# Layer norms whose mean and 1/deviation stay in PSUM, with the whole norm on VectorE and the rotary embedding of the folded halves behind it

## The chip, the cores and the metric

The kernel runs on one core of a Trainium2 chip. The metric is device time in microseconds (us), from the start of the kernel to its end. Five engines work side by side, each through its own queue in order: TensorE (PE; its weight loads are listed as PEld), VectorE (DVE), ScalarE (ACT), GpSimd (POOL) and SyncE (SP), which here only issues loads. An engine waits where its next instruction needs something that another has not finished. [...]

## The reference: one inference step of a two-layer decoder

288 tokens (256 of a prompt, 8 sequences of 4 new tokens) go through two layers of width 1024 in float32. Each layer is

```
proj = x @ w_in                        # 768 q, 768 k, 768 v, 2 x 256 of the gate
q, k = rope(q), rope(k)                # rotary embedding of 16 of 64 dimensions
mix  = [dilated window attention (3 groups of 4 heads, with caches), spatial gate]
x = layer_norm(alpha * x + mix @ w_mix_out)
x = layer_norm(alpha * x + cross_attention(x @ w_xq, memory) @ w_xo)
x = layer_norm(alpha * x + square(relu(x @ w_up)) @ w_down)

def layer_norm(x, g, b):               # over the 1024 features of a token
    mu, var = mean(x), mean((x - mu) ** 2)
    return (x - mu) / sqrt(var + 1e-5) * g + b
```

## The kernel before

Activations lie transposed: 8 tiles of 128 features by 288 tokens. `linear` walks over tiles of 256 columns of a weight matrix, two halves of 128 columns each. Weights and inputs are split into a high part (rounded to the fast matmul format) and the rest, and a half-tile is 24 matmuls into one PSUM bank `acc`: high by high, low by high and high by low, for each of 8 feature tiles (L336 to L338). `acc` has three banks, used in turn, so half-tile n waits until the evacuation of half n-3 has read its bank. ScalarE makes the high part `wh` of the weights (L318), VectorE the low part `wl` (L319); three buffers of each, so they run two halves ahead.

A layer norm needs all 1024 features before its first output. So the linear behind it starts with **folded** halves, which run on (z - c) * g, not normalised yet (`fH`, `fL`), with c a first estimate of the mean; two more columns give the terms in g and b, hence 290 columns. `LN.stats` multiplies the sums with a matrix of ones (L562, L563), so that every partition has mean and mean square; ScalarE copies the mean to SBUF (`s`, L565) and makes 1/deviation (`q`, L569, L570). `LN.fold` then evacuates a folded half: `fw` is copied out of the bank (L501), `fy` = s * fw + acc on VectorE (L502, the last to read the bank), and `fy` *= q (L505), on GpSimd for the first four of a norm and on VectorE later. `LN.apply` makes the normalised x itself: subtract the mean (L577, tiles in turn on VectorE and GpSimd), scale by g and 1/deviation (L581, VectorE), high part `xH` and the shift by b on ScalarE (L584, L586), low part `xL` on VectorE (L591).

There are five such norms: ahead of `w_xq` in both layers (xq norm: all eight halves folded, and no `xH` or `xL` made), ahead of `w_up` in both (up norm: three tiles, six halves folded) and ahead of `w_in` of the second layer (w_in norm: two tiles, four halves folded; these are queries). In `w_in` the evacuation of q and k halves ends with the rotary embedding: shuffle and product on VectorE (L671, L672), product and sum on GpSimd (L673, L674). From the rotated queries of a group ScalarE makes `zq`, `zn`, and a `query` goes by memory (`qd`, `qb`) onto the partitions of the cached keys, where VectorE and GpSimd multiply them (L1009, L1007).

The order on each engine comes from a scheduler that interleaves such tasks by priorities and modelled latencies; `behind` holds an instruction back until an urgent one has been queued (`gates`).

## Time and profile before

| | us |
|---|---|
| median of 3 runs | 1097.1 (1093.85 to 1100.27) |
| span of the profiled execution | 1090.5, 6.6 below the median of the runs |
| PE busy | 1045.1 (96%) |
| DVE busy | 767.2 (70%) |
| ACT busy | 534.1 (49%) |
| POOL busy | 191.2 (18%) |
| means issued (L562) | 170.71, 329.61, 538.71, 709.82, 868.50 |

The profile shows one execution. The span runs from the first to the last instruction; no other time of that execution is given. The five times in the last row are where the norms stand: xq, up, w_in, xq, up.

### The profile page before, as it was taken

What the parts mean: (1) busy time and instruction counts of PE and PEld (TensorE: products, weight loads), DVE (VectorE), ACT (ScalarE), POOL (GpSimd) and SP (SyncE); (2) the same over time, 40 slices, a digit from 0 to 9 for tenths busy, and PEclk for the clock granted to TensorE, in tenths of its full rate; (3) what the DMA queues carried; (4) which work ended last, traced back from release to release, by engine and by line L of the source; (5) the groups of instructions that cost most, each with busy time, mean ns of one, the idle gap of its engine ahead of it and who ended that gap; (6) DMA issues with size and microseconds to landing.
All of it is one profiled execution on the core that took longest, in us unless ns stands there. A gap on an engine that the chain in (4) does not pass through costs nothing. (4 is left out here: it accounts for less than half of the span.)

```text
span 1090.5 us, 20141 instructions
## 1 busy us (share of the span) xinstructions
PE 1045.1 (96%) x8038; PEld 957.0 (88%) x8038; DVE 767.2 (70%) x1406; ACT 534.1 (49%) x1000; POOL 191.2 (18%) x151
## 2 busy tenths in 40 slices
PE   8989999999999999999978998999999999999995
PEld 7979599878898999999968885997788999999995
DVE  6688689755479756565998876895554997565656
ACT  4437456544457535353553373674343585354432
POOL 5592022000023000000469300220000320000000
PEclk9999999999999999999989999999999999999998
DMA  9988955687854655545446869456865555555531
GB/s 291 303 249 280 244 185 189 205 256 236 299 160 136 194 161 186 156 157 172 136 128 214 250 209 265 155 192 201 276 209 206 155 146 184 160 171 183 182 117 43
DMA packets 185533, 213.68 MB, mean 196 GB/s; under 512 B 5760, under 2 KB 175136, under 8 KB 185440
## 3 DMA queue, kind: packets, MB, share of 16 engines
q1 hardware_dynamic: 177216, 205.00, 59.9%
q10 hardware_dynamic: 8224, 7.41, 2.1%
q8 instruction: 63, 1.03, 0.4%
q14 instruction: 30, 0.25, 0.1%
HBM read 203.80 MB, written 8.59 MB: 195 GB/s over the span
## 5 line engine op out<-in xcount | busy, mean ns | idle before, releaser
L318 ACT ACTIVATE wh<-wraw 128x1024 fp32r<-128x1024 f32 (+1 forms) x237 | 249.4, 1054 | 294.9 <-PE acc L337 218.8
L319 DVE TENSOR_TENSOR wl<-wraw,wh 128x1024 fp32r<-128x1024 f32 (+1 forms) x237 | 309.1, 1306 | 113.2 <-ACT wh L318 112.1
L336 PE MATMUL acc<-xH,wh 128*128 128x288 f32 x728 | 218.5, 301 | 6.8 <-DVE fy L502 6.8
L338 PE MATMUL acc<-xH,wl 128*128 128x288 f32 x728 | 217.5, 299 | 3.3 <-DVE wl L319 3.3
L337 PE MATMUL acc<-xL,wh 128*128 128x288 f32 x728 | 217.5, 299 | 0.0
L336 PE MATMUL acc<-hH,wh 128*128 128x288 f32 x512 | 151.3, 296 | 0.0
L337 PE MATMUL acc<-hL,wh 128*128 128x288 f32 x512 | 151.2, 295 | 0.0
L338 PE MATMUL acc<-hH,wl 128*128 128x288 f32 x512 | 150.9, 295 | 0.0
L336 PEld LDWEIGHTS acc<-xH,wh 128*128 128x128 f32 x728 | 138.6, 191 | 8.2 <-issue 5.2
L338 PEld LDWEIGHTS acc<-xH,wl 128*128 128x128 f32 x728 | 138.5, 191 | 4.8 <-DVE wl L319 4.2
L337 PEld LDWEIGHTS acc<-xL,wh 128*128 128x128 f32 x728 | 138.6, 190 | 1.0 <-DVE fy L726 0.4
L520 POOL TENSOR_TENSOR s<-s,xres 128x288 f32<-128x288 f32 x15 | 20.3, 1353 | 464.4 <-DVE s L516 463.9
L336 PEld LDWEIGHTS acc<-hH,wh 128*128 128x128 f32 x512 | 96.3, 188 | 0.0
L337 PEld LDWEIGHTS acc<-hL,wh 128*128 128x128 f32 x512 | 96.3, 188 | 0.0
L338 PEld LDWEIGHTS acc<-hH,wl 128*128 128x128 f32 x512 | 96.2, 188 | 0.0
L336 PE MATMUL acc<-fH,wh 128*128 128x290 f32 x256 | 78.1, 305 | 1.8 <-DVE fy L502 1.8
L337 PE MATMUL acc<-fL,wh 128*128 128x290 f32 x256 | 77.0, 301 | 0.0
L338 PE MATMUL acc<-fH,wl 128*128 128x290 f32 x256 | 75.7, 299 | 0.5 <-DVE wl L319 0.5
L336 PEld LDWEIGHTS acc<-fH,wh 128*128 128x128 f32 x256 | 48.3, 189 | 2.6 <-PE acc L338 2.2
L337 PEld LDWEIGHTS acc<-fL,wh 128*128 128x128 f32 x256 | 48.5, 190 | 0.9 <-DVE fL L494 0.2
L338 PEld LDWEIGHTS acc<-fH,wl 128*128 128x128 f32 x256 | 48.1, 189 | 1.2 <-DVE wl L319 1.0
L1007 POOL TENSOR_TENSOR cu<-cu,qb 128x1024 f32<-128x1024 f32 x15 | 44.1, 2956 | 11.1 <-DMA qb<-qd 10.7
(318 smaller groups left out, 2199.4 us busy)
## 6 DMA issues: line engine op xcount, KB each, us to landing
cu<-cache_mem_kv SPq DMA_DIRECT2D x64, 512.0 KB, 6.2
wraw<-w_up SPq DMA_DIRECT2D x32, 1024.0 KB, 5.5
wraw<-w_down SPq DMA_DIRECT2D x32, 1024.0 KB, 4.9
cu<-cache_kv_w SPq DMA_DIRECT2D x48, 512.0 KB, 6.4
wraw<-w_in SPq DMA_DIRECT2D x21, 1024.0 KB, 6.7
wraw<-w_xkv SPq DMA_DIRECT2D x16, 1024.0 KB, 5.6
wraw<-w_mix_out SPq DMA_DIRECT2D x8, 1024.0 KB, 6.0
wraw<-w_xq SPq DMA_DIRECT2D x8, 1024.0 KB, 5.0
```

The costliest lines, as they stand in the source:

```text
L318: S.activation(h[:, r], raw[:, r], AF.Copy)
L319: gates[f"split{k}"] = behind(V.tensor_sub(lo[:, r], raw[:, r], h[:, r].bitcast(F32)), "dve")
L336: m = T.matmul(ps, wh[:, k], H[:, k], start=first, stop=False)
L337: T.matmul(ps, wh[:, k], L[:, k], start=False, stop=False)
L338: T.matmul(ps, wl[:, k], H[:, k], start=False, stop=last)
L520: eng.tensor_add(self.s, self.s, xres[:, n])
L1007: G.tensor_mul(cu, cu, qb[g])
```

## The change

Mean and 1/deviation stay in the PSUM tiles that the statistics make (`pd`, `pq`, now of the pool `dec`, which has two banks, and no longer of `tr`), and 1/deviation is written there by ScalarE. GpSimd no longer takes part: all eight subtractions and every fold's multiplication are VectorE's. `apply` is no longer a generator that hands on tile by tile: it issues all subtractions, all scalings with `xH`, then all `xL`, which now come straight from x + b - xH. The shift of x by b comes two tiles later (`shift_back`). In `w_in` the evacuations' second part (bias and rotary embedding) of the folded halves is held until all of `apply` is issued. The first half on `xH` takes its matmuls in another order, low part of x last. The scores of the decode attention wait for `apply`, since they use the other `dec` bank.

```diff
     def linear(name, l, k0, tiles, H, L, N, evac, norm=None, folded=0, apply_at=1, ks=range(KT)):
+        held = []
         for i, c in enumerate(tiles):
             if i == apply_at and folded:
-                for _ in norm.todo:
-                    pass
+                norm.apply(H, L)
+            if i == folded:
+                for args in held:
+                    evac(*args)
+            if i == apply_at + 2 and folded:
+                norm.shift_back()
...
+                elif i == folded and not a and folded:
+                    for j, (u, v) in enumerate(((wt[0], h), (wt[1], h), (wt[0], lo))):
+                        for k in range(KT):
+                            T.matmul(p[:, :cols], u[:, k], v[:, k], start=(j + k == 0), stop=(j + k == KT + 1))
...
-                    evac(2 * c + a, *norm.fold(p))
+                    args = (2 * c + a, *norm.fold(p))
+                    if name == "w_in":
+                        held.append(args)
+                    else:
+                        evac(*args)
...
         def fold(self, ps):
...
-            self.folds += 1
-            (G if self.folds <= FOLD_POOL else V).tensor_mul(e, e, self.q)
+            V.tensor_mul(e, e, self.rstd)
...
         def stats(self):
-            pd, pq = tr(), tr()
-            T.matmul(pd[:, :TOK], ones, self.s, start=True, stop=True)
-            gates["pe"] = T.matmul(pq[:, :TOK], ones, self.q, start=True, stop=True)
-            m2, rstd = self.c, self.q
-            S.activation(self.s, pd[:, :TOK], AF.Copy)
-            S.activation(m2, pd[:, :TOK], AF.Square)
-            gates["dve"] = V.scalar_tensor_tensor(out=m2, in0=pq[:, :TOK], scalar=EPS, in1=m2,
+            pd, pq = dec("pd"), dec("pq")
+            self.mean, self.rstd = pd[:, :TOK], pq[:, :TOK]
+            T.matmul(self.mean, ones, self.s, start=True, stop=True)
+            gates["pe"] = T.matmul(self.rstd, ones, self.q, start=True, stop=True)
+            m2 = self.c
+            S.activation(m2, self.mean, AF.Square)
+            gates["dve"] = V.scalar_tensor_tensor(out=m2, in0=self.rstd, scalar=EPS, in1=m2,
                                                   op0=ALU.add, op1=ALU.subtract)
+            S.activation(self.s, self.mean, AF.Copy)
             S.activation(m2, m2, AF.Ln)
-            gates["act"] = S.activation(rstd, m2, AF.Exp, scale=-0.5)
+            S.activation(self.rstd, m2, AF.Exp, scale=-0.5)

         def apply(self, H, L=None):
...
-            for i in range(KT + 2):
-                if i < KT:
-                    (V if i in SUB_V else G).tensor_sub(xres[:, i], xres[:, i], self.s)
-                n = i - 1
-                if 0 <= n < KT:
...
+            for n in range(KT):
+                if n in SUB_V:
+                    behind(V.tensor_sub(xres[:, n], xres[:, n], self.mean), "dve")
...
+            for n in range(KT):
+                x, b = xres[:, n], lncol(j, 1, l, n)
+                V.scalar_tensor_tensor(out=x, in0=x, scalar=lncol(j, 0, l, n), in1=self.rstd,
+                                       op0=ALU.mult, op1=ALU.mult)
+                if H is not None:
+                    S.activation(H[:, n], x, AF.Identity, bias=b)
+            if L is not None:
+                for n in range(KT):
+                    V.scalar_tensor_tensor(out=L[:, n], in0=xres[:, n], scalar=lncol(j, 1, l, n),
+                                           in1=H[:, n].bitcast(F32), op0=ALU.add, op1=ALU.subtract)
+            tasks.flag("applied", 0)
+
+        def shift_back(self):
+            for n in range(KT):
+                S.activation(xres[:, n], xres[:, n], AF.Identity, bias=lncol(self.j, 1, self.l, n))
...
         def decode_scores():
-            sc = dec("sc")
...
+            yield "applied"
+            sc = dec("sc")
```

How this moves instructions shows in the order of the queues. Line numbers differ between the two kernels (L502 is L512 in the changed one, L319 L317, L581 L593, L577 L588, L591 L599).

The first place is VectorE's queue in the up norm of the first layer. Before, the evacuations of the folded halves two to four (of `acc_3903`, `acc_3984`, `acc_4023`) stand right behind the scalings and ahead of every low part `xL`:

```order
L581 SCALAR_TENSOR_TENSOR xres_103<-xres_103,lnp_155,q_3506 128x288 x8
L501 COPY fw_3928<-acc_3903 128x2
L319 TENSOR_TENSOR wl_3981<-wraw_3746,wh_3980 128x1024
L1383 TENSOR_TENSOR r_3870<-r_3870 128x288
L501 COPY fw_4009<-acc_3984 128x2
L502 SCALAR_TENSOR_TENSOR fy_3929<-s_3505,fw_3928,acc_3903 128x288
L319 TENSOR_TENSOR wl_4020<-wraw_3746,wh_4019 128x1024
L1384 TENSOR_TENSOR hL_3833<-r_3870,hH_3832 128x288
L501 COPY fw_4048<-acc_4023 128x2
L502 SCALAR_TENSOR_TENSOR fy_4010<-s_3505,fw_4009,acc_3984 128x288
L502 SCALAR_TENSOR_TENSOR fy_4049<-s_3505,fw_4048,acc_4023 128x288
```

In the changed kernel the queue, from the low parts on, reads so up to the evacuation of the fourth folded half, now `acc_4015`:

```order
L512 SCALAR_TENSOR_TENSOR fy_4002<-s_3505,fw_4001,acc_3976 128x288
L317 TENSOR_TENSOR wl_4053<-wraw_3834,wh_4052 128x1024
L599 SCALAR_TENSOR_TENSOR xL_3831<-xres_103,lnp_155,xH_3830 128x288
L1397 TENSOR_TENSOR r_3933<-r_3933 128x288
L599 SCALAR_TENSOR_TENSOR xL_3831<-xres_103,lnp_155,xH_3830 128x288 x3
L511 COPY fw_4081<-acc_4056 128x2
L599 SCALAR_TENSOR_TENSOR xL_3831<-xres_103,lnp_155,xH_3830 128x288
L514 TENSOR_TENSOR fy_4002<-fy_4002,pq_3822 128x288
L317 TENSOR_TENSOR wl_4092<-wraw_3834,wh_4091 128x1024
L599 SCALAR_TENSOR_TENSOR xL_3831<-xres_103,lnp_155,xH_3830 128x288 x3
L1398 TENSOR_TENSOR hL_3833<-r_3933,hH_3832 128x288
L511 COPY fw_4120<-acc_4095 128x2
```

The row behind these twelve is `fy_4041`, which reads `acc_4015` (and the rows ahead of them are the scalings, eight in a row). The fourth evacuation has moved from ahead of the low parts to behind all eight of them and two more `wl`; its bank is the one that the seventh half, the first on `xH`, takes.

The second place is VectorE's queue in the w_in norm. Before, each rotary embedding (`ro`) stands between the evacuations, and the fourth (`fy_6331`) behind three of them and four low parts:

```order
L671 STREAM_SHUFFLE ro_6213<-fy_6207 128x288
L672 TENSOR_TENSOR ro_6212<-fy_6207,const_63 128x288
L502 SCALAR_TENSOR_TENSOR fy_6290<-s_5550,fw_6289,acc_6264 128x288
L591 TENSOR_TENSOR xL_6124<-xres_103,xH_6123 128x288 x3
L726 TENSOR_SCALAR fy_6290<-fy_6290,fw_6289 128x288
L591 TENSOR_TENSOR xL_6124<-xres_103,xH_6123 128x288
L671 STREAM_SHUFFLE ro_6296<-fy_6290 128x288
L672 TENSOR_TENSOR ro_6295<-fy_6290,const_63 128x288
L502 SCALAR_TENSOR_TENSOR fy_6331<-s_5550,fw_6330,acc_6305 128x288
```

In the changed kernel the evacuations two to four (`fy_6199`, `fy_6267`, `fy_6302`) have come forward and the first rotary row stands behind the fourth:

```order
L512 SCALAR_TENSOR_TENSOR fy_6267<-s_5550,fw_6266,acc_6241 128x288
L514 TENSOR_TENSOR fy_6199<-fy_6199,pq_6115 128x288
L593 SCALAR_TENSOR_TENSOR xres_103<-xres_103,lnp_155,pq_6115 128x288 x8
L511 COPY fw_6301<-acc_6276 128x2
L514 TENSOR_TENSOR fy_6267<-fy_6267,pq_6115 128x288
L317 TENSOR_TENSOR wl_6345<-wraw_6133,wh_6344 128x1024
L741 TENSOR_SCALAR fy_6199<-fy_6199,fw_6198 128x288
L599 SCALAR_TENSOR_TENSOR xL_6124<-xres_103,lnp_155,xH_6123 128x288 x6
L512 SCALAR_TENSOR_TENSOR fy_6302<-s_5550,fw_6301,acc_6276 128x288
L684 STREAM_SHUFFLE ro_6316<-fy_6165 128x288
```

All four rotary embeddings of the folded halves now follow one after another behind this piece, with the shuffles of the next two halves behind them and the next `wl` (`wl_6380`) behind those.

The third place is ScalarE's queue there. Before, `xH` is followed by shifts of x, with the copies of the rotated queries in between:

```order
L318 ACTIVATE wh_6356<-wraw_6133 128x1024
L584 ACTIVATE xH_6123<-xres_103,lnp_155 128x288 x8
L586 ACTIVATE xres_103<-xres_103,lnp_155 128x288 x3
L963 COPY zq0_86<-qT_6125 64x2x4x4
L945 COPY zn_91<-qT_6125 64x32 x2
L586 ACTIVATE xres_103<-xres_103,lnp_155 128x288 x5
```

In the changed kernel the next high part of the weights, `wh_6379`, stands behind all shifts and both copies:

```order
L596 ACTIVATE xH_6123<-xres_103,lnp_155 128x288 x8
L605 ACTIVATE xres_103<-xres_103,lnp_155 128x288 x8
L979 COPY zq0_86<-qT_6125 64x2x4x4
L959 COPY zn_91<-qT_6125 64x32 x2
L979 COPY zq0_86<-qT_6125 64x2x4x4
L959 COPY zn_91<-qT_6125 64x32 x2
L316 ACTIVATE wh_6379<-wraw_6133 128x1024
```

What moved is little: the same copies stood ahead of the same part of the weights before, but the rotary embeddings whose result they copy stand further back in VectorE's queue.

## Rows read from the trace of the kernel before

**Rows 1.** The page: the span, and each engine's busy time, share and instructions.
```profile
span 1090.5 us, 20141 instructions
PE 1045.1 (96%) x8038; PEld 957.0 (88%) x8038; DVE 767.2 (70%) x1406; ACT 534.1 (49%) x1000; POOL 191.2 (18%) x151
```

**Rows 2.** The waits of PE: what, for whom, us in total, times, longest.
```profile
PE acc L336 <- DVE fy L502: 8.6, 4, 4.9
```

**Rows 3.** Timeline of PE, first layer's up norm: start, us, instruction, [idle before].
```profile
329.61 0.48 PE L562 MATMUL tr<-s,const 128*128 128x288 f32 x1 [0.78 <-DVE s L520]
...
331.17 0.38 PE L1183 MATMUL tr<-const,late 128*128 128x128 f32 x2
...
336.04 0.40 PE L338 MATMUL acc<-fH,wl 128*128 128x290 f32 x1 [0.27 <-DVE wl L319]
...
343.37 0.37 PE L336 MATMUL acc<-fH,wh 128*128 128x290 f32 x1 [0.90 <-DVE fy L502]
...
349.92 0.30 PE L336 MATMUL acc<-xH,wh 128*128 128x288 f32 x1
```

**Rows 4.** Timeline of PE, linear behind the w_in norm.
```profile
553.79 0.37 PE L336 MATMUL acc<-xH,wh 128*128 128x288 f32 x1 [1.96 <-DVE fy L502]
559.01 0.58 PE L336 MATMUL acc<-xH,wh 128*128 128x288 f32 x1 [4.85 <-DVE fy L502]
...
595.72 0.40 PE L989 MATMUL tr<-const,qT 128*32 128x128 f32 x1 [3.06 <-POOL qT L674]
...
619.12 0.61 PE L338 MATMUL acc<-xH,wl 128*128 128x288 f32 x1 [2.64 <-DVE wl L319]
```

**Rows 5.** Windows: us, busy by engine (PE, PEld, DVE, ACT, POOL), granted clock, DMA.
```profile
341.00:345.00 4.00, 3.10 (x23) 2.88 (x23) 4.00 (x10) 3.87 (x9) 1.69 (x1) 1.00 0.85 283
...
562.00:564.00 2.00, 2.00 (x9) 2.00 (x10) 2.00 (x7) 0.00 (x0) 1.52 (x2) 0.50 0.00 0
564.00:566.00 2.00, 2.00 (x15) 1.64 (x13) 1.30 (x4) 0.00 (x0) 2.00 (x2) 0.93 0.00 0
...
598.00:600.00 2.00, 2.00 (x16) 1.99 (x16) 2.00 (x3) 0.07 (x1) 1.92 (x3) 0.89 1.06 331
...
622.00:624.00 2.00, 2.00 (x19) 2.00 (x19) 2.00 (x2) 0.00 (x0) 0.00 (x0) 0.92 0.34 107
```

**Rows 6.** Timeline of DVE, first layer's up norm.
```profile
330.84 2.42 DVE L577 TENSOR_TENSOR xres<-xres,s 128x288 f32<-128x288 f32 x3
...
334.53 3.20 DVE L319 TENSOR_TENSOR wl<-wraw,wh 128x1024 fp32r<-128x1024 f32 x2
337.66 3.51 DVE L581 SCALAR_TENSOR_TENSOR xres<-xres,lnp,q 128x288 f32<-128x288 f32 x8
...
342.66 0.15 DVE L501 COPY fw<-acc 128x2 f32<-128x2 f32 x1
```

**Rows 7.** One operation's instructions: ns min/median/max, first and last start.
```profile
L577 DVE TENSOR_TENSOR xres<-xres,s x20: 447/849/1072, 171.9 to 872.5; 128x288 f32<-128x288 f32 x20
...
L581 DVE SCALAR_TENSOR_TENSOR xres<-xres,lnp,q x40: 501/506/511, 178.8 to 879.6; 128x288 f32<-128x288 f32 x40
...
L319 DVE TENSOR_TENSOR wl<-wraw,wh x237: 687/1225/3415, 11.6 to 1067.0; 128x1024 fp32r<-128x1024 f32 x118, 128x512 fp32r<-128x512 f32 x1
...
L527 DVE TENSOR_TENSOR xres<-xres,acc x28: 435/442/453, 155.7 to 867.4; 128x288 f32<-128x288 f32 x28
```

**Rows 8.** Window over the first layer's xq norm, columns as in rows 5.
```profile
164.00:200.00 36.00, 35.84 (x264) 34.17 (x263) 35.50 (x64) 23.94 (x44) 7.75 (x8) 1.00 0.59 192
```

**Rows 9.** Timeline of ACT in the w_in norm.
```profile
552.26 3.50 ACT L584 ACTIVATE xH<-xres,lnp 128x288 fp32r<-128x288 f32 x8
```

**Rows 10.** Timeline of POOL behind the w_in norm.
```profile
578.93 9.17 POOL L1007 TENSOR_TENSOR cu<-cu,qb 128x1024 f32<-128x1024 f32 x3 [1.60 <-DMA qb<-qd]
...
593.90 1.77 POOL L674 TENSOR_TENSOR qT<-ro 128x288 f32<-128x288 f32 x1
...
612.23 5.75 POOL L1007 TENSOR_TENSOR cu<-cu,qb 128x1024 f32<-128x1024 f32 x2 [7.18 <-DMA qb<-qd]
```

More of the change, by code (lines that the diff above doesn't have):

```diff
@@ L55 @@
 SCALED_G = True
-XRES_ACT = (0, 1, 2, 3, 4, 5, 6, 7)
 QUERY_2 = 4
-FOLD_POOL = 4
 MN_DVE = (0,)
@@ L63 @@
 CP_PRIO = (2, 1, 3)
-SUB_V = (0, 2, 4, 6)
+SUB_V = range(8)
 GELU_C = float(np.sqrt(2.0 / np.pi))
@@ L478, in __init__ @@
             self.H = None
-            self.folds = 0
         def fold_input(self, n):
@@ L569, in stats @@
             S.activation(m2, m2, AF.Ln)
-            gates["act"] = S.activation(rstd, m2, AF.Exp, scale=-0.5)
+            S.activation(self.rstd, m2, AF.Exp, scale=-0.5)
         def apply(self, H, L=None):
             j, l = self.j, self.l
-            for i in range(KT + 2):
-                if i < KT:
-                    (V if i in SUB_V else G).tensor_sub(xres[:, i], xres[:, i], self.s)
-                n = i - 1
-                if 0 <= n < KT:
-                    x, b = xres[:, n], lncol(j, 1, l, n)
-                    V.scalar_tensor_tensor(out=x, in0=x, scalar=lncol(j, 0, l, n), in1=self.q,
-                                           op0=ALU.mult, op1=ALU.mult)
-                    if H is not None:
-                        S.activation(H[:, n], x, AF.Identity, bias=b)
-                    if n in XRES_ACT:
-                        S.activation(x, x, AF.Identity, bias=b)
-                    else:
-                        G.tensor_scalar(x, x, b, None, op0=ALU.add)
-                n = i - 2
-                if n >= 0 and L is not None:
-                    V.tensor_sub(L[:, n], xres[:, n], H[:, n].bitcast(F32))
-                yield 0, 900
+            for n in range(KT):
+                if n in SUB_V:
+                    behind(V.tensor_sub(xres[:, n], xres[:, n], self.mean), "dve")
+                else:
+                    G.tensor_sub(xres[:, n], xres[:, n], self.s)
@@ L681, in layer @@
         flag = tasks.flag
+        if norm is None:
+            flag("applied", 0)
         qT = slot([128, 6, TOK], name="qT")
@@ L1171, in evac_q @@
             S.activation(dst, ps[:, 256:288].rearrange("p (b t) -> p b t", t=4), AF.Identity, bias=bias)
-        ln.todo = ln.apply(None)
         tasks.run(linear("w_xq", l, 0, range(4), None, None, TOK, evac_q, norm=ln, folded=4), 0.3)
@@ L1362, in layer @@
         xL = slot([128, KT, TOK], F32R, name="xL")
-        ln.todo = ln.apply(xH, xL)
         for h in range(LATE, 4):
@@ L1413, in layer @@
             xL = slot([128, KT, TOK], F32R, name="xL")
-            ln.todo = ln.apply(xH, xL)
             return xH, xL, ln
```

## The prediction

> **What bounds the kernel now.** I read the page first, then TensorE's chain of waits, then the timelines around the five norms whose code changes, stage by stage. TensorE is busy 96% of the span, VectorE 70%, ScalarE 49%, GpSimd 18% [rows 1], so a change can pay only where TensorE stands still, and costs wherever it makes TensorE wait. The longest total in the chain of waits is TensorE waiting for VectorE's `fy` at L502: 8.6 us in four waits [rows 2]. That is the evacuation of a folded half: `acc` has three banks, so half-tile n cannot start before the evacuation of half n-3 has read its bank.
>
> Two stages hold nearly all of it. In the **up norm** (layer 0 shown, layer 1 alike) the matmul of the mean, L562, which I call `pd` by its name in the change, is issued at 329.61, a wait of 0.27 for a `wl` stands at 336.04, a bank wait of 0.90 at 343.37, and the first half that uses the normalised `xH` starts at 349.92, so 20.31 us behind `pd` [rows 3]. In the **w_in norm** the bank waits are 1.96 and 4.85 us; later in that linear TensorE waits 3.06 us for GpSimd's rotary result and 2.64 us for a `wl` [rows 4]. [...]
>
> **The prices.** The eight `L581` took 3.51 us together, one alone 0.506: (3.51-0.51)/7 = 0.43 us from issue to issue, so 0.08 less than a duration [rows 6, 7]. By the same 0.08 a subtraction of 0.447 counts 0.37, a `wl` of 1.225 counts 1.14, an `fw` copy 0.07. Beside GpSimd these rise: three `L577` took 2.42 where 1.2 were due, two `wl` 3.20 where 2.36 were due [rows 6].
>
> No row shows a subtraction or a multiplication of the norm with its operand in PSUM. Below: the subtraction alone, 447 ns; above: 849, its median beside GpSimd. I take 447, since L527, an addition of the same tile with one operand in PSUM, has a median of 442 [rows 7]. [...]
>
> **Up norm, twice.** The new order puts all eight subtractions, then all eight scalings, then the low parts in front of the evacuation of the fourth folded half, whose bank the first `xH` half needs. GpSimd's part moves over too: four subtractions and the multiplications. What stands on VectorE from the first `fy` (about 1.5 us after `pd`, 0.3 behind the place of the first subtraction before, 330.84 [rows 6], since the copy of the mean now follows the square on ScalarE) up to that fourth `fy` is: six `wl` (6.84), eight subtractions (2.96), eight scalings (3.44), eight low parts (3.44), four `fy` (1.72), one `c` (0.37), three `fy` multiplications (1.11), two `r` and two `hL` (1.48), five `fw` (0.35): 21.7 us. The bank is free 23.2 us after `pd`. TensorE's own work up to there is 20.31 less its two waits of 0.27 and 0.90, and less some 0.65 for six transposes (three pairs like that at 331.17 [rows 3]) that now run ahead of `pd`: 18.5 us; with up to 1.5 us of shorter bank waits on the way it is ready at 20. So a wait of 3 to 4 us stands where there was none, and the half starts 2.9 us later behind `pd`, and `pd` itself about 0.6 later by the transposes. In length the wait is like the one of 3.06 us, so half clock follows: 1.25 (as after 3.06) to 2.5 (as after 4.85); I take 1.8. Sum 2.9+0.6+1.8 = **5.3 us**, two norms **+10.6** (bounds 7 to 14). From there TensorE is the bound again, and nothing gives it back.
>
> **xq norm, twice.** VectorE is busy 35.5 of 36 us there [rows 8]. It gets four subtractions (1.5) and four multiplications (1.5) more, and is rid of what GpSimd cost it (1.2 at the subtractions, 0.84 at the `wl`, about as much again at later `wl`). All tiles are folded, so no `xH` is waited for. A wait of about 1 us behind the scalings is offset by transposes moved ahead. **+0.5** for both (bounds -1 to +2).
>
> **w_in norm, once.** The ropes of the four folded halves now stand behind the low parts, and the evacuations ahead of them. The 1.96 and 4.85 us go. In their place: VectorE ends the subtractions and three `fy` later, its first scaling about 12.3 us after `pd`, so TensorE, done with the folded halves at about 10.5 to 11.4, waits 1.6 to 2.5 us for the first `xH`, then runs at ScalarE's pace (eight in 3.50 [rows 9]) to about 16.5. Then it runs on the low parts until about 25, where it waits some 3 to 5 us: the next `wl` stands behind six ropes on VectorE, and its `wh` on ScalarE behind `zq` and `zn`, which wait for GpSimd's first two rope results, now begun only at about `pd` + 21. Against before, which started these halves at `pd` + 20.3 and at half clock, I work out a lead of some 4 us (3 to 6) at 570. Next late is GpSimd: the query leaves 2 to 4 us later, its three multiplications of 9.17 us [rows 10] end at about 591, and the rotary result that the next transposes need comes at 595 to 597, as late as the one at 593.90 + 1.77 before [rows 10]; but TensorE has by then some 35 matmuls more behind it, 4.7 us at 0.136 each (from 343.37 to 349.92 two halves of 24 took 6.55 [rows 3]), of which the later result takes 0 to 1.3: 3.9 kept. In the new order the `wl` that was missing at 619.12 stands ahead of the multiplication that waits for the second query, so 2.64 and 1.5 of half clock go as well; the `wl` of three halves later stands behind it. The second query (landed 612.2 before [rows 10]) is issued some 4 us later and lands at 610 to 617; that `wl` follows some 9 us behind (GpSimd's two multiplications, 5.75 [rows 10], then three reductions and the `wl` itself), and TensorE waits 0 to 6 us. So 3.9 + 4.1 less about 1.5: **-6.5** (bounds -1 to -10). The tail to 677 is fed by loads that start with TensorE's work, and moves along.
>
> **Sum.** +10.6 + 0.5 - 6.5 = **+4.6 us** on the profiled span of 1090.5 [rows 1], so 1095.1. The median of the runs is 1097.1, 6.6 above the span; with these 6.6 unchanged the forecast is **1101.5 us**, own range 1097 to 1106. About 0.5% (5.5 us, so 1091.6 and 1102.6) is what a measurement here can tell from no change.
>
> **Rivals.**
> *No new wait in the up norm* (faster). VectorE, with GpSimd silent, would have to be through its list in 17 us in place of 21.7. For it: the pair of `wl` beside GpSimd took 0.84 more than two alone, the subtractions 1.2. Against: I count all at that lower price already, and the number of instructions is fixed by the order. Then the 0.27 and 0.90 go (-2.3 for two), and 1097.1 - 2.3 + 0.5 - 6.5 = **1088.8**.
> *The lead in w_in is given back* (slower). If the second query lands at 620 or later, or k's rope result at 600, TensorE only waits longer at the same places, with half clock again; the gain shrinks to about 1: 1097.1 + 10.6 + 0.5 - 1 = **1107.2**. For it: both hang on GpSimd, which runs at 9.17 for three multiplications and starts its ropes later than before; against: the `wl` at 619 is moved out of it.
> *Operands in PSUM are dearer.* At the upper bound each of the eight subtractions takes 849 in place of 447 ns: 3.2 us more ahead of the bank in each up norm and as much ahead of the first `xH` in w_in, 1101.5 + 9.6 = **1111.1**. It decides from about 0.05 us an operation on, which brings the forecast past 1102.6. Against: 442 against 447 ns [rows 7]; for it no row. [...]
>
> **How the numbers follow.** Forecast 0.45; no new wait 0.15; lead given back 0.25; operands dearer 0.05; the other 0.10 goes to a w_in norm that gains 10 or more, half of it with up norms at their lower bound, 1089 to 1096. Of the forecast's own 0.45 three tenths lie above 1102.6. Slower: 0.25 + 0.05 + 0.13 = 0.43. Faster: 0.15 + 0.05 = 0.20. Within 0.5%: 0.37. The range goes from just under the faster rival to above the slower one with a full half-clock loss: 1088 to 1110.
>
> **What would show it.** Right: in both up norms a wait of 3 to 4 us for VectorE's `fy` right ahead of the first `xH` matmul, at 23 us behind `pd`, with a granted clock near 0.5 after it; in w_in no wait of 4.85, a wait for `xH` of about 2 us, one of 3 to 5 for the rope chain, and none at the 17th half. Wrong: an `xH` half in the up norm that starts within 21 us of `pd` (the first rival), subtractions and scalings of over 0.5 us (the third), or a w_in linear that ends no earlier against its `pd` than before (the second).

## The result and the profile after

The changed kernel took 1109.39 us (median of 4 runs, 1107.66 to 1114.23), the one before 1098.68 in the same comparison: ratio 1.0101, interval 1.0063 to 1.0140, so slower by 1%. The profiled execution is the one of 1114.23, the slowest of its four, while the span of before, 1090.5, lies at the short end of its own; what their 21.6 us of difference in span hold beyond the median's 10.7 is read with care below.

The page of the changed kernel, span and busy times, answers to [rows 1]:

```profile
span 1112.1 us, 20099 instructions
PE 1055.6 (95%) x8038; PEld 966.2 (87%) x8038; DVE 770.3 (69%) x1446; ACT 535.8 (48%) x1000; POOL 147.6 (13%) x111
```

GpSimd is relieved of 44 us and VectorE has 3 more. The waits of PE in the changed kernel (us in total, times, longest), beside [rows 2]:

```profile
PE o L1091 <- DMA cu<-cache_kv_w: 12.5, 7, 6.9
PE acc L363 <- DVE fy L512: 7.8, 2, 3.9
PE acc L334 <- DVE fy L512: 3.5, 4, 0.9
PE acc L363 <- ACT xH L596: 1.7, 1, 1.7
```

The second line is the forecast wait of the up norm, twice 3.9. The first is not in the forecast at all: the products with cached values at the end of the decode attention (L1091, L1075 before) wait for their loads. Of the 12.5 us, 10.5 lie in the last such products of the stage behind the w_in norm, called its tail below. The same list for 640 to 705 us alone, changed kernel first, then before:

```profile
PE o L1091 <- DMA cu<-cache_kv_w: 10.5, 5, 6.9
```

```profile
PE o L1075 <- DMA cu<-cache_kv_w: 2.2, 2, 1.6
```

The timeline of PE in the first layer's up norm, beside [rows 3]:

```profile
327.76 0.51 PE L573 MATMUL pd<-s,const 128*128 128x288 f32 x1
...
340.36 0.37 PE L334 MATMUL acc<-fH,wh 128*128 128x290 f32 x1 [0.92 <-DVE fy L512]
...
344.68 0.37 PE L334 MATMUL acc<-fH,wh 128*128 128x290 f32 x1 [0.83 <-DVE fy L512]
...
352.04 2.26 PE L363 MATMUL acc<-xH,wh 128*128 128x288 f32 x8 [3.91 <-DVE fy L512]
```

The first half on `xH` starts 24.28 us behind `pd`, 3.97 later than before. The windows there (columns as in [rows 5], the granted clock as a share of full speed) show half clock, 0.50, from 352 to 356, and 0.66 in the next 2 us; ten matmuls stand in 354 to 356, 17 in 358 to 360, at 1.00. With work taken to run at half speed at 0.50, the 1.96, 2.00 and 2.00 us busy at 0.50, 0.50 and 0.66 are an estimated 2.7 us lost. Ahead of it TensorE had stood still for the 3.91:

```profile
352.00:354.00 2.00, 1.96 (x8) 1.99 (x9) 2.00 (x4) 0.32 (x2) 0.00 (x0) 0.50 1.02 325
354.00:356.00 2.00, 2.00 (x10) 2.00 (x9) 1.97 (x6) 1.66 (x4) 0.00 (x0) 0.50 0.31 110
356.00:358.00 2.00, 2.00 (x12) 2.00 (x12) 1.41 (x4) 0.75 (x3) 0.00 (x0) 0.66 0.00 0
358.00:360.00 2.00, 2.00 (x17) 2.00 (x17) 0.72 (x1) 1.91 (x4) 0.00 (x0) 1.00 0.00 0
```

What the operands in PSUM cost, from the durations of the subtraction, the scaling and the fold's product (ns min/median/max), the first two beside [rows 7], the third beside the row of before that stands below it:

```profile
L588 DVE TENSOR_TENSOR xres<-xres,pd x40: 448/451/455, 174.8 to 890.0; 128x288 f32<-128x288 f32 x40
...
L593 DVE SCALAR_TENSOR_TENSOR xres<-xres,lnp,pq x40: 508/512/523, 182.1 to 899.8; 128x288 f32<-128x288 f32 x40
...
L514 DVE TENSOR_TENSOR fy<-fy,pq x32: 444/455/468, 177.7 to 912.3; 128x288 f32<-128x288 f32 x32
```

```profile
L505 DVE TENSOR_TENSOR fy<-fy,q x12: 449/454/461, 191.0 to 891.2; 128x288 f32<-128x288 f32 x12
```

451 stands against 447 with both operands in SBUF, 512 against 506, 455 against 454.

In the w_in norm (mean at 543.67) PE's timeline has the forecast wait for `xH`, then waits for the rotary chain; the third row shown is the longest wait in the tail:

```profile
556.54 0.40 PE L363 MATMUL acc<-xH,wh 128*128 128x288 f32 x1 [1.71 <-ACT xH L596]
...
572.54 0.40 PE L1005 MATMUL tr<-const,qT 128*32 128x128 f32 x1 [1.19 <-DVE ro L685]
...
684.16 0.66 PE L1091 MATMUL o<-cu,z 128*32 128x256 f32 x4 [6.93 <-DMA cu<-cache_kv_w]
```

GpSimd's timeline shows when the two queries were there, 47.2 and 82.0 us behind the mean; before it was 40.2 and 73.5 [rows 10]:

```profile
590.86 10.05 POOL L1023 TENSOR_TENSOR cu<-cu,qb 128x1024 f32<-128x1024 f32 x3 [3.76 <-DMA qb<-qd]
...
625.70 6.72 POOL L1023 TENSOR_TENSOR cu<-cu,qb 128x1024 f32<-128x1024 f32 x2 [14.97 <-DMA qb<-qd]
```

And SyncE's queue in the tail, changed kernel first, then the one before. The load of the memory (`mem_nat`, 1 MB, needed only in the next phase) has moved ahead of the last six loads of cached values. No line of the change says so; the scheduler's modelled times did it.

```profile
658.59 5.97 SPq L138 DMA_DIRECT2D cu<-cache_kv_w  x7
664.66 0.56 SPq L1158 DMA_DIRECT2D mem_nat<-mem_prompt  x1
665.85 9.67 SPq L138 DMA_DIRECT2D cu<-cache_kv_w  x6
```

```profile
652.01 14.69 SPq L140 DMA_DIRECT2D cu<-cache_kv_w  x13
667.19 0.37 SPq L1142 DMA_DIRECT2D mem_nat<-mem_prompt  x1
```

All stages together, as differences of the times of the five means (us; "e" names the experiments below, one profiled execution each):

| | ratio (interval) | to 1st mean | xq | up | w_in | xq | up to end |
|---|---|---|---|---|---|---|---|
| before | | 170.7 | 158.9 | 209.1 | 171.1 | 158.7 | 222.0 |
| after | 1.0101 (1.0063-1.0140) | 169.7 | 158.1 | 215.9 | 183.4 | 156.9 | 228.1 |
| e1 after again | 1.0121 (1.0076-1.0166) | 172.4 | 158.0 | 214.9 | 178.5 | 157.1 | 228.1 |
| e2 load behind | 1.0093 (1.0061-1.0126) | 172.1 | 158.0 | 216.0 | 173.6 | 157.7 | 226.4 |
| e3 folds first | 1.0061 (1.0035-1.0087) | 170.9 | 158.1 | 211.6 | 179.0 | 158.5 | 223.7 |
| e4 ropes not held | 1.0101 (1.0062-1.0141) | 173.1 | 157.9 | 216.0 | 172.8 | 157.7 | 227.7 |
| e5 folds first, full | 1.0046 (1.0018-1.0075) | 176.8 | 157.9 | 211.9 | 180.9 | 157.9 | 224.3 |
| e6 stats in `tr` | 1.0075 (1.0046-1.0105) | 170.7 | 160.0 | 213.0 | 173.4 | 159.3 | 225.7 |
| e7 GpSimd subtracts | 1.0098 (1.0062-1.0134) | 170.7 | 157.6 | 214.3 | 178.8 | 156.6 | 225.8 |
| e8 xq alone | 0.9989 (0.9966-1.0012) | 173.7 | 158.1 | 209.3 | 172.9 | 158.1 | 222.0 |
| e9 w_in alone | 1.0062 (1.0034-1.0089) | 172.6 | 158.9 | 209.9 | 177.0 | 159.8 | 222.0 |
| e10 w_in alone, load behind | 1.0007 (0.9980-1.0033) | 169.0 | 159.0 | 210.1 | 174.4 | 158.5 | 221.8 |
| e11 up alone | 1.0102 (1.0050-1.0155) | 173.0 | 158.8 | 215.3 | 178.0 | 158.6 | 227.0 |
| e12 xq and up, folds first | 1.0067 (1.0038-1.0096) | 171.1 | 158.1 | 211.5 | 179.3 | 158.1 | 224.2 |

The xq stages repeat to within about 1 us for the same code, the up stages to within 2: behind the wait of 3.9 us the clock is at 0.50 for 6.8 us in some places and for 3.4 in others (e11 has both, 6.8 in the first layer and 3.4 in the second). The first stage, whose code no kernel here changes, spreads over 8 us. The w_in stage spreads for the same code too: 183.4 and 178.5 in two executions of the changed kernel. It is judged by medians, not by one profile. The runs were taken in three groups, e1 to e4, e5 to e8 and e9 to e12, each with runs of the kernel before beside it (medians 1098.17, 1097.61 and 1094.68); between groups the ratios compare, not the times.

The stages are cut at the means, and they do not hold the same work everywhere. Where the new norm stands, the scheduler moves transposes ahead of the mean that stood behind it, and so into the stage before: 20 of cached values (`cu`, 2.0 us of TensorE's time) at each xq norm, 16 of them (1.5 us) at the w_in norm, six (0.6 us) at each up norm. e6 moves none. The last twelve of the 20 ahead of the second xq norm in e12:

```profile
718.41 1.47 PE L965 MATMUL tr<-const,cu 128*128 128x128 f32 x12
```

### The profile page after: what moved, and what is told of

The parts are those of the page before. It is cut to its first block, busy times and chain, and to the rows that moved or that the text cites. A ratio compares the mean times of both kernels' runs of the same rounds, so it can differ in the third digit from the quotient of the medians.

```text
span 1112.1 us, 20099 instructions
## 1 busy us (share of the span) xinstructions
PE 1055.6 (95%) x8038; PEld 966.2 (87%) x8038; DVE 770.3 (69%) x1446; ACT 535.8 (48%) x1000; POOL 147.6 (13%) x111
## 5 line engine op out<-in xcount | busy, mean ns | idle before, releaser
L317 DVE TENSOR_TENSOR wl<-wraw,wh 128x1024 fp32r<-128x1024 f32 (+1 forms) x237 | 299.8, 1268 | 122.4 <-ACT wh L316 121.7
L334 PE MATMUL acc<-xH,wh 128*128 128x288 f32 x704 | 211.3, 301 | 2.7 <-DVE ro L685 2.0
L336 PE MATMUL acc<-xH,wl 128*128 128x288 f32 x704 | 209.7, 299 | 1.0 <-DVE wl L317 1.0
L335 PE MATMUL acc<-xL,wh 128*128 128x288 f32 x704 | 209.6, 298 | 0.0
L334 PEld LDWEIGHTS acc<-xH,wh 128*128 128x128 f32 x704 | 134.0, 190 | 3.9 <-ACT zn L959 2.1
L336 PEld LDWEIGHTS acc<-xH,wl 128*128 128x128 f32 x704 | 133.4, 190 | 2.1 <-DVE wl L317 1.5
L335 PEld LDWEIGHTS acc<-xL,wh 128*128 128x128 f32 x704 | 134.3, 191 | 0.0
L1023 POOL TENSOR_TENSOR cu<-cu,qb 128x1024 f32<-128x1024 f32 x15 | 46.4, 3110 | 20.2 <-DMA qb<-qd 18.7
```

Of the source, the lines that this page charges most:

```text
L317: gates[f"split{k}"] = behind(V.tensor_sub(lo[:, r], raw[:, r], h[:, r].bitcast(F32)), "dve")
L334: m = T.matmul(ps, wh[:, k], H[:, k], start=first, stop=False)
L335: T.matmul(ps, wh[:, k], L[:, k], start=False, stop=False)
L336: T.matmul(ps, wl[:, k], H[:, k], start=False, stop=last)
L1023: G.tensor_mul(cu, cu, qb[g])
```

## The experiments

**e1, the changed kernel again** (no edit), for the long wait in the tail.

> The changed kernel once more, unaltered. In its first trace one megabyte of mem_prompt is issued ahead of the last six loads of cached values in the second layer, and TensorE waits 6.93 us for one of them; the kernel before issues it behind them. Theory A (this order of the loads is part of the loss): the wait comes again, over 5 us at 110 to 145 us behind the third pd, ratio about 1.010. Rival B (that wait was a chance of one execution): no wait over 2.5 us there, and the span is 1106 or less.

1111.41 us. The tail's waits for cached values were 5.0 us, the longest 3.0, so 6.93 was partly that execution's own; the span was 1108.9. Neither text was met in full: there is a wait there in both executions, but its length varies.

**e2, the load of the memory held behind the last load of cached values.**

```diff
+            if self.order[self.issued][0] != "mem":
+                self.pv = ins
...
+            gates["pv"] = cs.pv
+        behind(m, "pv")
```

> The changed kernel with the load of mem_prompt held behind the last load of cached values; nothing else is asked for. Theory A: the stretch from the first to the last product with cached values falls from 35.0 to about 27 us (26.3 before the change), the long wait there goes, and the time falls by 5 to 9 us against the changed kernel: ratio to the kernel before 1.002 to 1.006. Rival C (the loads themselves start late, because the second query lands late): the stretch stays at 33 us or more, the ratio at 1.009 or more.

1106.87 us. The tail's longest wait is 1.9 us (4.6 in all) and from the first to the last product of the tail it is 22.7 us (34.4 in the changed kernel, 28.8 in e1, 25.1 before). So the stretch fell as theory A had it, but the medians gain 2.5 to 4.5 us, less than expected, the ratio of 1.0093 is the one of rival C, and the intervals overlap. e9 and e10 separate the load better.

**e3, the up norm issued one tile later**, on top of e2, so that all evacuations of folded halves up to the fourth stand ahead of the subtractions.

```diff
-FOLD_UP, APPLY_UP = 3, 1
+FOLD_UP, APPLY_UP = 3, 2
```

> e2_load_behind, and in the up norms apply is issued after the fourth folded half in place of the second, so that the evacuations of all four stand ahead of the scalings and low parts on VectorE. Theory D (the wait for the fourth evacuation costs 5 to 7 us in each up norm): the waits of 0.9, 0.8 and 3.9 us ahead of the first xH half go, half clock there too, the half starts within 20.5 us of pd, and the time is 9 to 13 us below e2_load_behind: ratio about 0.993. Rival E (VectorE is simply too full there): the wait turns into one of about the same length for xH, for xL or for a wl, and less than 4 us are won.

In this kernel `shift_back` falls behind the last tile and the shift of x by b is left out in both up norms (16 ScalarE operations). 1103.16 us: both waits of 3.9 us are gone, the first matmul on `xH` stands 19.2 us behind the mean, with waits of 0.42 us for `fy` and 0.19 for `xH` behind it. (In e12, with this order in the kernel before, the clock is at 0.50 for 3.4 us from 22.6 behind the mean, after 2 us with four matmuls in them.) The stages fall by 4.4 and 2.7 us against e2, the median by 3.7: by the waits theory D is right about the place, by the gain the kernel lies in the rival's range of under 4.

**e4, rotary embeddings not held**, on top of e2.

```diff
-                    if name == "w_in":
-                        held.append(args)
-                    else:
-                        evac(*args)
+                    evac(*args)
```

> e2_load_behind, and in w_in the rotary embeddings of the folded halves are no longer held behind apply. Theory F (holding them makes both queries late and gives the lead back): both queries land earlier than at 590.8 and 625.6 less the shift of pd, by 4 us or more, but the evacuation of the fourth folded half is behind ropes again, with a wait of 3 us or more for it; the w_in stage from pd to pd of the next norm is shorter than in e2_load_behind by 2 us or more. Rival G (holding is a gain as forecast): the stage is longer by 2 us or more.

1107.5 us. The second query is used 70 us behind the mean, 12 earlier than in e2, but other waits come in its place, as PE's list shows:

```profile
PE acc L338 <- DVE wl L319: 5.3, 2, 3.7
PE acc L365 <- ACT xH L595: 4.2, 1, 4.2
...
PE sc L962 <- POOL kT L686: 2.9, 1, 2.9
```

The stage is 172.8 against 173.6. So neither the hold nor the query alone is seen to set it; both texts missed.

**e5, e3 with the shift in its place.**

```diff
-            if i == apply_at + 2 and folded:
+            if i == 3 and folded:
```

> As e3_up_folds_first, which left out the shift of x by b in both up norms (16 ScalarE operations); here the shift is back, at the third tile. Theory D: the shift lies beside other work, the waits of 0.8 and 3.9 us ahead of the first xH half stay away with their half clock, up stage at about 211.6 us against 216.0 with the load behind alone, ratio about 1.005. Rival E (e3 was fast because the shift was left out): the up stage is back above 214 us.

1102.66 us, a ratio of 1.0046 where e3 has 1.0061, the up stages 211.9 and 224.3. The left-out operations of e3 were not what it gained.

**e6, the statistics back in the pool `tr`**, on top of e2; the decode scores then wait for nothing.

```diff
-            pd, pq = dec("pd"), dec("pq")
+            pd, pq = tr("pd"), tr("pq")
...
-            yield "applied"
```

> e2_load_behind with mean and 1/deviation in the PSUM pool that they had before the change, so the scores of the decode attention need not wait for apply and the transposes of the cached keys stand behind pd again. Theory H (it is the late start of the key work, by way of the pool, that costs in w_in): the w_in stage from pd to pd, with the up stage ahead of it taken together, falls by 3 us or more against e2_load_behind (216.0 + 173.6 = 389.6). Rival I (the late ropes and queries set it): the sum stays within 2 us, and the second query's products still start 80 us or more behind pd.

1106.26 us. The first `xH` half of the up norm still starts 24.6 us behind the mean, after two shorter waits (2.28 and 1.25). In the sum of the up and w_in stages it is 3.2 us shorter than e2, which is theory H's figure, but 1.4 of that are transposes that e2 has moved into these stages from their neighbours: from the first mean to the end the two take 931.4 and 931.7 us. In the ratios (1.0075 and 1.0093) no difference shows either.

**e7, four subtractions on GpSimd again**, on top of e2; VectorE's four still read the mean from PSUM.

```diff
-SUB_V = range(8)
+SUB_V = (0, 2, 4, 6)
```

> e2_load_behind with four of the eight subtractions of each norm back on GpSimd, which reads the mean from SBUF, while VectorE's four read it from PSUM. Theory J (contention is between operations that both read two operands from SBUF): VectorE's subtractions take 0.45 us beside GpSimd's in place of the 0.85 before the change, only the weights' low parts beside them are slow, and the first xH half of the up norm starts 0.5 to 1.5 us earlier than 24.3 us behind pd. Rival K (GpSimd slows VectorE whatever it reads): subtractions of 0.8 us or more, and the half starts as late or later.

1110.17 us. VectorE's subtractions beside GpSimd's four, and GpSimd's own:

```profile
L590 DVE TENSOR_TENSOR xres<-xres,pd x20: 439/441/449, 176.4 to 882.5; 128x288 f32<-128x288 f32 x20
```

```profile
329.87 5.23 POOL L592 TENSOR_TENSOR xres<-xres,s 128x288 f32<-128x288 f32 x4 [6.64 <-ACT s L581]
```

The median is 441 ns and the longest 449, where the same operation beside GpSimd's four subtractions took 849 with the mean in SBUF [rows 7]; 18 of the 20 here overlap one of GpSimd's. That is theory J's figure and not rival K's; which reads contend is shown no further than by these two medians. The first `xH` half is 0.7 us earlier behind the mean, and its wait stays (3.88); the ratio, 1.0098, is no better than that of e2.

The last five kernels put the new norm into the kernel before, one kind of norm at a time or, in e12, two: `NEW` lists the kinds that get it (0 xq, 1 up, 2 w_in; e8 asks for kind 0 in the same places).

```diff
+            self.folds, self.new = 0, j in NEW
...
+                if norm.new:
+                    norm.apply(H, L)
+                else:
+                    norm.apply_old(H, L)
```

**e8, the xq norms alone.**

> The kernel before with the new norm in the two xq norms alone (PSUM residency, all on VectorE, shift later); up and w_in norms, and the order of the loads, as before. Theory L (the change is neutral to slightly good where every half is folded): the xq stages are 0.5 to 1.5 us shorter each, ratio 0.997 to 1.000. Rival M (any VectorE work more in that stage costs): stages longer by 0.5 us or more, ratio above 1.001.

1096.81 us; the xq stages are 158.1 and 158.1 against 158.9 and 158.7. The stages look shorter because 2.0 us of transposes have left each of them: w_in and the second xq stage together are 331.0 in e8 and 329.8 before. By the ratio it is neutral.

**e9, the w_in norm alone.**

> The kernel before, with the new norm (statistics in PSUM, all of it on VectorE, rotary embeddings behind it, decode scores behind it) in the w_in norm alone; its queue of loads has the load of the memory ahead of the last six of cached values, as in the changed kernel. Theory M (the w_in step loses by itself, through the tail that is fed by loads): the stage from the w_in norm's mean to the next norm's is 178 to 184 us against 171.1 before, the others stay within 2, and the ratio is 1.005 to 1.011. Rival N (the loss there comes only behind the changed up norm): that stage is at most 172 and the ratio at most 1.002.

1102.63 us against 1094.68 of before (29 runs, shared by e9 to e12). A loss by itself, but the stage in the profile is 177.0, just under what theory M gave.

**e10, the w_in norm alone, with the load of the memory held behind** (the edit of e2).

> The run above with the load of the memory held behind the last load of cached values. Theory M says 172 to 176 us for that stage and a ratio of 1.001 to 1.005, the rest of the loss being the later queries. If the whole loss is the order of the loads: 168 to 171 and a ratio of at most 1.000, and the gain that was forecast would show, in part.

1095.44 us. The load's place, and what the scheduler alters around it in the tail, is worth 7.2 us of median between e9 and e10, whose intervals do not overlap. (Besides the load, operations of TensorE, VectorE and ScalarE stand in another order there.) In the two profiles only 2.6 of it lie in the w_in stage and 3.6 in the first one, and the tail's waits for cached values are not longer in e9 (2.2 us) than in e10; its products take 29.2 us against 23.7. So that this place of the load, with the order that comes with it, costs is shown by the times, but not by which wait. With the load behind, the new w_in norm neither gains nor loses. PE's waits of e10 in 640 to 705 us:

```profile
PE o L1131 <- DMA cu<-cache_kv_w: 4.5, 3, 2.9
```

**e11, the up norms alone.**

> The kernel before, with the new norm in both up norms alone. Theory P (the wait for the fourth folded half is a loss of its own): a wait of 3.5 to 4 us ahead of the first half on the normalised input, at 24 us behind the mean, both times, and half clock after it; the two stages behind the up norms grow from 209.1 and 222.0 to 213.5 to 215.5 and 226.5 to 228.5, the others within 1.5 of before, and the ratio is 1.008 to 1.012. Rival Q (part of that loss came in through w_in's new code): both stages grow by under 3 us and the ratio is at most 1.005.

1109.56 us. The waits are there as expected, of 3.87 and 3.88 us:

```profile
PE acc L336 <- DVE fy L518: 8.4, 5, 4.9
PE acc L368 <- DVE fy L518: 7.7, 2, 3.9
PE acc L338 <- DVE wl L319: 6.1, 2, 3.9
```

The up stages grow by 6.2 and 5.0. But the w_in stage was expected within 1.5 of before and took 178.0, although every engine's order of instructions there is that of before; the third row is part of it. The median is no clean measure of the up norms for that reason: four of the six runs lie from 1107.95 to 1112.44, two at 1099.21 and 1100.08. The last section follows that.

**e12, xq and up norms, folds first, w_in as before.**

> The kernel before, with the new norm in the xq and up norms, the up norms issued one tile later so that the fourth folded half is evacuated ahead of the subtractions; w_in as before. If the losses are the two places named so far and they add up, the stages behind the up norms are 209 to 212 and 222 to 224.5, w_in 170 to 172.5, and the ratio is 0.998 to 1.004. If moving the folds forward costs elsewhere (as the 1.0046 of the version with both moves might say), it is 1.004 or more.

1102.87 us, above the range of the first text except for its two shortest runs (1093.4 and 1095.8; the ten others lie from 1101.5 to 1106.4). The ratio is that of the second text, but the up stages are as the first has them (211.5, 224.2); w_in took 179.3 in the profiled execution, again with before's order up to the 2.0 us of transposes ahead of the next mean. No version beat the kernel before by what can be measured; e8 is level with it.

## Why the prediction was right, and where it was not

The forecast was 1101.5 us, 0.4% above its median (its terms add up to 1101.7); the kernel came out 1% slower, on the side given the highest chance. That it lies inside the range is in part luck: 1109.39 is 0.6 under the upper end of 1110, which was set for the second rival, and above the forecast's own 1097 to 1106, and e1, the same kernel again, has 1111.41. What was right is the up norm; the w_in norm, which was to give back more than half of that loss, gave nothing.

**Up norm: right, in mechanism and nearly in size.** Forecast +10.6 for both; in e11 the two stages grow by 6.2 and 5.0, together 11.2. (The ratio, 1.0102, is +11.2 us too, 5.5 to 17.0, but holds w_in's longer executions as well.) VectorE's list up to the fourth `fy`, that one included, was to take 21.7 us from 1.5 behind `pd`; in the changed kernel it starts at 329.30, 1.54 behind, with the very numbers of operations that were counted, and the fourth `fy` runs from 351.39 to 351.90, so 22.6 us. Two waits inside the list, which the step took as unbroken, are 0.6 of the 0.9 us:

```profile
337.26 1.23 DVE L317 TENSOR_TENSOR wl<-wraw,wh 128x1024 fp32r<-128x1024 f32 x1 [0.26 <-ACT wh L316]
...
338.83 0.46 DVE L1397 TENSOR_TENSOR r<-r 128x288 f32<-128x288 f32 x1 [0.35 <-ACT hH L1396]
```

The half starts at 24.28 in place of 23.2, so 4.0 later than before and not 2.9. The clock cost an estimated 2.7 us, a little over the upper value of 2.5 and not the 1.8 taken; e1 and e2 have one norm each with half as long at 0.50. (The prediction's losses by the clock, 1.25 and 2.5 here and 1.5 in w_in, are estimates from [rows 4] and [rows 5]: the windows have the clock back 2.7, 5.3 and 3.2 us behind 595.72, 559.01 and 619.12, and half of that is 1.4, 2.6 and 1.6.) The 0.6 for the six transposes moved ahead of `pd` did not come: before, TensorE stood still for 0.78 us ahead of `pd` [rows 3], and they fill that. So the sum was right within 1 us per norm because terms too small and one too large met. e3 and e5 show that the order makes the wait. The first rival (no wait) fails on the 24.28.

**xq norm: right within the noise.** Forecast +0.5 for both (-1 to +2); e8 gives -1.2 (-3.7 to +1.3), which holds the forecast and zero.

**Prices: right.** The third rival, dearer operands in PSUM, fails on 451 against 447, 512 against 506 and 455 against 454 ns. (Its sign, subtractions and scalings of over 0.5 us, was badly set for the scalings, which took 506 ns before.) The trace shows 1 to 6 ns more.

**w_in norm: wrong in sign.** Forecast -6.5 (-1 to -10); e9 gives +6.8 (3.7 to 9.7), e10, without the moved load, +0.8 (-2.2 to +3.6). The early steps held: a wait for `xH` of 1.71 (forecast 1.6 to 2.5), no wait of 4.85, none at the 17th half. The wait for the rotary chain was 1.19, not 3 to 5. Counting this linear's matmuls from the mean, TensorE in the changed kernel is 10 us ahead of before at 24 us, 6.3 at 32, 3.8 at 45, 1.0 at 74, 5.5 at 80 and 2.5 at 90. The lead of 4 was about right; that 3.9 of it are kept behind the rotary results was not, since TensorE waits 1.97 and 0.83 us there (57.0 and 58.4 behind the mean) and has a granted clock of 0.50 from 59.5 to 66. The step that failed outright is the last: "The tail to 677 is fed by loads that start with TensorE's work, and moves along." The tail's products need the softmax over the second query's scores, and that query was used at 82.0 in place of 73.5 behind the mean. At 620, the bound of the second rival, it would have been 81.3. The scaling of the softmax's probabilities comes at 104.3 behind the mean in place of 100.6, the first product at 114.2 in place of 112.6. So the lead is gone before the tail starts, in e10 too (103.5 and 114.2). That is the outcome of the second rival, whose 1107.2 is nearer to 1109.39 than the forecast is. Its sign, a linear that ends no earlier behind its mean than before, did not come, though: the last matmul of the linear ends 105.9 us behind the mean in the changed kernel and 108.5 in e10, in place of 109.9, so the loss shows only behind the linear. (TensorE's other work stands in another order, so that these ends alone do not measure a lead.) In the tail TensorE then waits 4.5 us for cached values (e10) where before waited 2.2; that the work done ahead is missing there as cover is argued, not tested.

Behind these waits the clock falls, which no step had. One window each of the tail of the changed kernel, of e10 and of before:

```profile
688.00:690.00 2.00, 2.00 (x14) 1.37 (x7) 0.00 (x0) 0.00 (x0) 0.00 (x0) 0.50 0.46 148
```

```profile
678.00:680.00 2.00, 2.00 (x9) 2.00 (x9) 0.21 (x1) 0.00 (x0) 0.00 (x0) 0.50 1.03 412
```

```profile
650.00:680.00 30.00, 27.83 (x242) 15.74 (x241) 19.15 (x74) 12.83 (x39) 0.00 (x0) 1.00 0.91 235
```

It is at 0.50 from 682 to 692 in the changed kernel, behind the wait of 6.93, and from 676.6 to 683.3 in e10, behind one of 2.87. In e10's profile this alone is of the size of what the stage loses: its last product with cached values ends 138.5 us behind the mean, before 138.3, and from there to the next mean, for the same work, e10 takes 3.1 us more; the 6.20 us that TensorE is busy from 676.6 to 683.3, at 0.50, are an estimated 3.1 us lost.

To that comes the moved load, which no step had: the queues of VectorE and ScalarE were laid side by side ahead of the prediction, SyncE's was not.

e4 keeps this from being the whole cause: with the query 12 us earlier other waits took its place. Shown is that the lead is gone by the tail; that the late query alone ends it is only argued.

**The sum.** Forecast 10.6 + 0.5 - 6.5. The parts alone measure 11.2 - 1.2 + 6.8 = 16.8, the whole 11 to 13. Parts that share the varying w_in stage don't add up exactly, and the intervals of the parts, some 3 to 6 us each way, allow it.

## What to carry to other kernels

List everything that stands on an engine between the statistics of a norm and the last read of a bank, in the order in which the queue holds it, and compare it with what TensorE has to do until it needs that bank: this count gave the wait to within 1 us. Follow a lead to the end of its stage, and ask at each joint what that stage waits for other than TensorE's own progress: a query's trip by memory (here used 8.5 us later), a load's place in the queue (7.2 us of median between e9 and e10, with the order that comes with it) or half clock behind a wait (an estimated 3.1 us in e10) may take it all. After any change in a scheduled kernel compare the queue of loads as well as the compute engines' queues; a load that nobody waits for yet can stand in front of one that is needed, as `mem_nat` here stands in front of six loads of cached values. And before stages of two kernels are compared, see that the same work lies between their ends.

## What the runs showed of the hardware that was not expected

**A clock that returns 0.6 us later, and what follows in that execution.** Behind the w_in norm e12 and before have the same instructions in the same order on every engine up to 164 us behind the mean, and the same wait of 4.85 us (at 20.3 us behind the mean). Their windows differ for the first time when the clock comes back, 25.3 to 26.3 us behind the mean in both: 0.85 before, then 0.55 in e12.

```profile
564.00:565.00 1.00, 1.00 (x9) 1.00 (x7) 0.91 (x3) 0.00 (x0) 1.00 (x1) 0.85 0.00 0
```

```profile
566.00:567.00 1.00, 1.00 (x7) 1.00 (x6) 0.90 (x3) 0.00 (x0) 1.00 (x1) 0.55 0.00 0
```

0.85 means that 0.3 of this microsecond ran at half clock, 0.55 that 0.9 did: TensorE is an estimated 0.3 us late. VectorE's next `wl` then starts 30.23 instead of 29.95 us behind the mean and takes 1.81 instead of 1.32 (before first, then e12):

```profile
568.66 1.32 DVE L319 TENSOR_TENSOR wl<-wraw,wh 128x1024 fp32r<-128x1024 f32 x1
```

```profile
570.94 1.81 DVE L319 TENSOR_TENSOR wl<-wraw,wh 128x1024 fp32r<-128x1024 f32 x1
```

GpSimd's next product for the rotary embedding starts 30.15 us behind the mean in both. Before, where the `wl` came first, the product took 1.79 us; in e12, where the product came first, it took 0.81 and the `wl` was the one that took longer. Two more executions agree: in e8 the `wl` starts at 29.97 and takes 1.29, the product 1.79; in e11 it starts at 30.28 and takes 1.75, the product 0.81.

The `wl` frees the buffer of the next weights load, which therefore leaves 0.8 us later, while the query's load and the weights load behind it leave at the same time as before (31.3, 32.5 and 38.0 us behind the mean before; 32.1, 32.5 and 38.0 in e12):

```profile
570.00 0.37 SPq L140 DMA_DIRECT2D wraw<-w_in  x1
571.20 0.64 SPq L996 DMA_DIRECT2D qb<-qd  x1
576.70 0.38 SPq L140 DMA_DIRECT2D wraw<-w_in  x1
```

```profile
572.78 0.37 SPq L140 DMA_DIRECT2D wraw<-w_in  x1
573.24 0.64 SPq L1050 DMA_DIRECT2D qb<-qd  x1
578.71 0.38 SPq L140 DMA_DIRECT2D wraw<-w_in  x1
```

The query is used 42.0 us behind the mean, not 40.2 (that its transfer runs further into that of the following weights is read off the order, not tested), and TensorE's waits for `wl` behind it are 2.09 and 3.74 us, with half clock after them (0.52 and 0.63 in the 4 us from 590.71, 0.50 from 622.71 to 630.71):

```profile
582.72 9.12 POOL L1061 TENSOR_TENSOR cu<-cu,qb 128x1024 f32<-128x1024 f32 x3 [3.36 <-DMA qb<-qd]
```

```profile
622.96 0.61 PE L338 MATMUL acc<-xH,wl 128*128 128x288 f32 x1 [3.74 <-DVE wl L319]
```

At 93 us e12 is 4.5 us behind before by the count of matmuls, at 164 us 6.6; the rest of the 8.2 at the end of the stage are the transposes moved into it. e11 shows the same steps (0.79 in 573 to 574, its query at 42.1, a stage of 178.0), and e8, with the clock back as early as before (0.84), has its query at 40.4 and a stage of 172.9, of which 2.0 are such transposes. Four executions agree, then, but in none was the clock's return set, so that it starts all this is read off the order in time. That it is what parts e12's ten longer runs from its two shorter ones is likely but not shown, and why a new up norm should bring the late return more often stays open.

**Operands in PSUM** cost VectorE 1 to 6 ns an operation. Beside GpSimd's four subtractions the two-input subtraction took 441 ns with the mean in PSUM (e7) and 849 with both inputs in SBUF (before).
